# Writing the output projection of a hybrid decoder between the attention's steps, six matmuls at a time

## The chip, the core and the metric

The kernel runs on one core of a Trainium2 chip. The metric is device time in microseconds (us) of one launch. The engines are TensorE (PE in the rows; PEld are its weight loads), VectorE (DVE), ScalarE (ACT), GpSimd (POOL) and SyncE (SP), which issues the DMA transfers.

## The reference, cut to what matters

Two layers run over 2048 prompt tokens and 64 sample tokens, with D_MODEL 1024. In each layer four branches of width 256 (differential attention, spatial gating, convolution, gated recurrence) are gated, joined and sent through one 1024x1024 output projection. What the change touches is the prompt's attention and that projection:

```python
def _diff_attend(q1, q2, k1, k2, v, qpos, kpos, lam):
    def probs(q, k):
        s = jnp.einsum('bqhd,bkhd->bhqk', q, k) * scale
        return jax.nn.softmax(jnp.where(visible, s, NEG_BIG), axis=-1)
    p = probs(q1, k1) - lam * probs(q2, k2)
    return jnp.einsum('bhqk,bkhd->bqhd', p, v)
...
mixed = jnp.concatenate([o_a, o_b, o_c, o_d], -1) @ w_out[l]
y = _layer_norm(ALPHA * x + gate * mixed, ln_g[l], ln_b[l])
```

There are four heads, each with two score maps (q1 with k1, q2 with k2) of 32 columns and values of 64 columns.

## The kernel before, in words

A layer has two stages. The first computes the input projections and the other three branches and parks queries, keys, values and gated branches in device memory. The second is the attention stage: the prompt's causal attention, and the output projection beside it.

The 16 token tiles of 128 (t = 0 to 15) are taken in query blocks `qbs`: tiles 0-3, 4-7, 8-11, 12-13, 14-15. For each block `attention` goes over the four heads, and in a head over the block's tiles. One pass of tile t in one head is called a *row* here; there are 64 of them in a layer, 32 with t below 8 (short) and 32 long ones. A row does this:

- `attn_probs` takes each of the two maps in pieces of up to 1024 keys (one piece in a short row, two in a long one). A piece is two score matmuls into one of the two S buffers of PSUM (L669; the last piece adds the causal mask, L671), a maximum on VectorE (L673; a second piece joins maxima, L675), and the exponential on ScalarE (L677), which frees the S buffer. The sums are joined (L682, L684).
- the same function combines the two maps on VectorE: short operations on one number per token (L688, L689, L693), in a long row a scaling on ScalarE (L697), and then P1 + r P2 for each piece (L703 and, for the first piece of a long row, L698).
- `attn_value` transposes the combined piece in groups of four 128x128 blocks (L716), copies each group to SBUF on ScalarE (`ph`, L718) and multiplies it with the values into X (L721). It is called for a row after `attn_probs` of the following row. At a head's last tile it divides and normalises through a chain of short VectorE operations (`rsqrt`, L179 to L190), and stores the result.

`out_tile` is the output projection of one token tile. It loads gates and branches, multiplies (GpSimd L1340 for one half, VectorE L1346 for the other), splits the product into two fp32r parts (L110 on ScalarE, L172 on GpSimd), runs 48 matmuls in two groups of 24 into a z buffer (L1364 to L1366; there is one z buffer in this stage), and finishes with the residual, the norm and the store on VectorE, ScalarE and GpSimd (L1368 to L1382). The last block's two tiles (`last`) use the S buffers instead of z.

In the text of the program the four or two tiles of a block go through `out_tile` behind the attention of the next block, under `prio(KN['POUT'], ...)` with POUT = -500. The text isn't what the engines run: a list scheduler (`TCK = dict(schedule_with_timeline_sim=True)`) takes each engine's next instruction by the place in the text, which `prio` shifts, among those that its own timing model holds ready. `order` below stands for what it left in each engine's queue. Each queue runs in order.

Of the kernel before, what the change touches and what calls it, by code (L numbers as in the profile page):

```python
# [9 lines left out]
F32 = mybir.dt.float32  # L10
# [14 lines left out]
P = 128  # L25
# [43 lines left out]
def hymba_step_kernel(  # L69
# [9 lines left out]
    nc = tc.nc  # L79
# [19 lines left out]
    def prio(o, f, *a):  # L99
        if not o:  # L100
            return f(*a)
        with tc.high_priority(o):
            return f(*a)
# [514 lines left out]

        yield from for_tok(l, g, h, [(O_AV, 256)], consume)

    def attention(l, t0, nt, Lx, ap, act=None):

        S = scr[l]
        prev = None
        gq, oq = divmod(t0 * P, TG)
        nkc = -(-(t0 + nt) // 4)
        while len(pool.vst) < nkc:
            vt = (ap.v if pool.vst else ap.v0).tile([P, 4, 256], F32, name=nm("V"))
            load(vt, S.vs[len(pool.vst)].rearrange("(k p) c -> p k c", p=P))
            pool.vst.append(vt)  # L630
        vst = pool.vst
        for hd in range(4):
            rows = slice(hd * 64, (hd + 1) * 64)
            kst = []
            for c in range(0, nkc * 512, 512):
                gg, o = divmod(c, TG)
                kt = ap.k.tile([P, 2, 512], F32R, tag="K", name=nm("K"), bufs=NK)
                for q, part in enumerate((0, 0, 1, 1)):
                    load(kt[q * 32:(q + 1) * 32], S.ks[gg][part][rows, o:o + 512].rearrange("(m d) t -> d m t", m=2))
                kst.append(kt)  # L640
            qt = ap.q.tile([P, 2, 512], F32R, tag="Q", name=nm("Q"), bufs=2)
            for q, part in enumerate((0, 1, 0, 1)):
                load(qt[q * 32:(q + 1) * 32, :, 0:nt * P], S.qs[gq][part][rows, oq:oq + nt * P].rearrange("(m d) t -> d m t", m=2))
            ls = smp.tile([P, 4], F32, tag="ls", name=nm("ls"), bufs=3)
            acc = None
            for j in range(nt):
                pm = prio(KN['PPB'] if t0 else KN['PPB'], attn_probs, t0 + j, qt[:, :, j * P:(j + 1) * P], kst, ls[:, j:j + 1], Lx, ap)
                if prev is not None:
                    prio(KN['PAV'], prev)
                acc = Xt() if j == 0 else acc  # L650
                prev = (lambda *a: lambda: attn_value(*a, Lx, l, ap))(t0 + j, pm, vst, acc, ls, j, nt, hd, act)
        prev()

    def attn_probs(qi, qt, kst, l1, Lx, ap):

        nk = qi + 1
        npc = -(-nk // 8)
        stt = smp.tile([P, 16], F32, tag="stt", name=nm("stt"), bufs=3)
        Pm = []
        sizes = [min(8, nk - k0) * P for k0 in range(0, nk, 8)]  # L660
        col = lambda m, j: stt[:, m * 8 + j:m * 8 + j + 1]
        for m in range(2):
            pms = []
            for pc, n in enumerate(sizes):
                s = St()
                for o in range(0, n, 512):
# [11 lines left out]
                pms.append(p)  # L678
# [6 lines left out]
            Pm.append((pms, lt))  # L685
        (p1s, lt1), (p2s, lt2) = Pm
# [17 lines left out]
        return p1s  # L704

    def attn_value(qi, pm, vst, acc, ls, j4, nt, hd, act, Lx, l, ap):

        nk = qi + 1
        hs = slice(hd * 64, (hd + 1) * 64)
        for c in range(0, nk, 4):  # L710
            n = min(4, nk - c)
            p1 = pm[c // 8]
# [12 lines left out]
        if j4 < nt - 1:  # L725
# [591 lines left out]
    def out_tile(l, ti, O, last=False, act=None):  # L1317
# [7 lines left out]
        for half in (1, 0) if last else (0, 1):  # L1325
# [11 lines left out]
            for k0, k1 in ((2, 4), (0, 2)) if last and not half else ((0, 4),):  # L1337
# [9 lines left out]
                cpy('EOH', hi[:, cs], tmp[:, cs])  # L1347
                sub_lo(nc.vector if last and not half else pick('EOL'), lo[:, cs], tmp[:, cs], hi[:, cs])
                parts += [(O_K[half * 4 + k], f4(hi)[:, k, :], f4(lo)[:, k, :]) for k in range(k0, k1)]
        x = []  # L1350
        both = St() if last else None
        bs = smp.tile([P, 2, 6], F32, tag="obs", name=nm("obs"), bufs=2)
        for j in range(2):
# [9 lines left out]
            for i, (k, a, b) in enumerate(parts):  # L1363
                nc.tensor.matmul(po[0:M], a, wh[:, k, :], start=(i == 0), stop=False)  # L1364
                nc.tensor.matmul(po[0:M], a, wl[:, k, :], start=False, stop=False)  # L1365
                nc.tensor.matmul(po[0:M], b, wh[:, k, :], start=False, stop=(i == KT - 1))  # L1366
            t = O.op.tile([P, 512], F32, tag="xs", name=nm("t"), bufs=4)
            nc.vector.tensor_tensor(t[0:M], po[0:M], O.gate[0:M, js], ALU.mult)  # L1368
            nc.vector.scalar_tensor_tensor(xt[0:M], xt[0:M], ALPHA, t[0:M], op0=ALU.mult, op1=ALU.add)
# [30 lines left out]
    for l in range(DEPTH):  # L1400
# [92 lines left out]
        with ExitStack() as ctx2, \  # L1493
# [5 lines left out]
            if KN['WF']:  # L1499
                O = prio(KN['PW'], out_weights, l, op)  # L1500

            qbs = [(t, 4) for t in range(0, NT - 4, 4)] + ([(NT - 4, 2), (NT - 2, 2)], [(NT - 4, 3), (NT - 1, 1)], [(NT - 4, 2), (NT - 2, 1), (NT - 1, 1)])[KN['QB']]
            pool.vst = []
            for i, qb in enumerate(qbs):
                act = op.tile([P, qb[1], 256], F32, name=nm("act")) if i == len(qbs) - 1 else None
                if i and KN['OT'] == 0:
# [3 lines left out]
                if i == 0:  # L1510
                    if not KN['WF']:
                        O = prio(KN['PW'], out_weights, l, op)
                    out_gate(l, O, True)
                    out_tile(l, None, O)
                    out_gate(l, O, False)
                elif KN['OT']:
                    for t in range(qbs[i - 1][1]):
                        prio(KN['POUT'], out_tile, l, qbs[i - 1][0] + t, O)
            for t in range(qbs[-1][1]):
                out_tile(l, qbs[-1][0] + t, O, True, act[:, t])  # L1520
        pool.T2 = None
        if l < DEPTH - 1:
            zpool = ExitStack()
# [42 lines left out]
```

## Time and profile before

| what | us |
|---|---|
| time, median of 3 runs (3178.14 to 3194.91) | 3178.37 |
| the profiled execution: its time | 3180.86 |
| its span in the trace | 3179.1 |
| attention stage of layer 0, first to last score matmul | 1039 to 1566 |
| what follows it, into layer 1's first projections | 1566 to 1640 |
| attention stage of layer 1, first to last score matmul | 2592 to 3121 |
| what follows it, to the end | 3121 to 3179 |

Times inside the trace count from the span's start. Idle time in a row of the profile is the time that the engine stood still just before the instructions of that row, with what ended it behind the arrow.

### The profile page before, as it was taken

Reading aid. Unit: us, or ns where it says so; the run is one execution under the profiler, and the core shown is the slowest. Engines: PE = TensorE matmul, PEld = TensorE weight load, DVE = VectorE, ACT = ScalarE, POOL = GpSimd, SP = SyncE. Lnnn points to the kernel's source line nnn. Section 1 sums busy time; section 2 is a strip of 40 time slices with the busy share of each in tenths; the row PEclk is TensorE's granted clock in tenths of the full one; section 3 lists DMA queues with packets and bytes.
Section 4 is the critical chain, followed back from the end, with each engine's and each line's share of the span. In section 5 each row is a group of like instructions: output and inputs, shape, how many; then the busy total and the mean of one; then the engine's idle time right before and its main releaser. Section 6 shows DMA issues by size and latency. Waiting matters only on the chain. (4 is left out here: it accounts for less than half of the span.)

```text
span 3179.1 us, 56041 instructions
## 1 busy us (share of the span) xinstructions
PE 2821.6 (89%) x20888; PEld 2254.3 (71%) x20888; DVE 2272.4 (71%) x5280; ACT 1224.7 (39%) x2564; POOL 1140.0 (36%) x1173
## 2 busy tenths in 40 slices
PE   5999979898999898888889999888999989988896
PEld 3888866788866566656678888667897756665665
DVE  3667873377693788989857769534768758888896
ACT  3212213312213666676542122232122246657663
POOL 3344464433231223313343444653323431332232
PEclk7999989999999898999989999999999989998998
DMA  6222323322336754366332232242232254434552
GB/s 210 67 76 91 92 75 115 87 64 82 120 124 209 184 130 126 107 152 162 106 119 75 78 98 77 85 127 65 68 117 73 70 169 123 132 101 111 156 152 69
DMA packets 342593, 353.26 MB, mean 111 GB/s; under 512 B 58575, under 2 KB 248565, under 8 KB 342306
## 3 DMA queue, kind: packets, MB, share of 16 engines
q1 hardware_dynamic: 336178, 332.89, 36.5%
q0 software_dynamic: 6144, 16.79, 1.8%
q8 instruction: 166, 2.72, 0.4%
q14 instruction: 105, 0.86, 0.1%
HBM read 266.44 MB, written 83.33 MB: 110 GB/s over the span
## 5 line engine op out<-in xcount | busy, mean ns | idle before, releaser
L516 PE MATMUL z<-hh,wh 128*128 128x512 f32 (+1 forms) x1440 | 527.9, 367 | 27.4 <-DVE zs L195 25.0
L518 PE MATMUL z<-hh,wl 128*128 128x512 f32 (+1 forms) x1440 | 521.0, 362 | 0.0
L517 PE MATMUL z<-hl,wh 128*128 128x512 f32 (+1 forms) x1440 | 520.9, 362 | 0.0
L172 POOL TENSOR_TENSOR wl<-raw,wh 128x512 fp32r<-128x512 f32 x224 | 317.6, 1431 | 552.7 <-ACT wh L110 496.8
L507 PE MATMUL z<-wh,hh 128*128 128x256 f32 (+1 forms) x1360 | 399.6, 294 | 12.4 <-ACT wh L110 4.5
L1017 DVE SCALAR_TENSOR_TENSOR acc<-glu,cw,acc 128x512 f32<-128x512 f32 x480 | 403.2, 885 | 3.3
L677 ACT ACTIVATE P<-S,stt 128x1024 f32<-128x1024 f32 (+7 forms) x384 | 332.9, 868 | 178.9 <-DVE stt L673 124.0
L673 DVE TENSOR_REDUCE stt<-S 128x1 f32<-128x1024 f32 (+7 forms) x384 | 345.0, 905 | 70.9 <-PE S L671 55.2
L508 PE MATMUL z<-wl,hh 128*128 128x256 f32 (+1 forms) x1360 | 393.9, 290 | 0.6 <-POOL wl L172 0.6
L509 PE MATMUL z<-wh,hl 128*128 128x256 f32 (+1 forms) x1360 | 394.3, 290 | 0.0
L516 PEld LDWEIGHTS z<-hh,wh 128*128 128x128 f32 x1440 | 275.3, 191 | 91.7 <-DVE zs L195 30.1
L518 PEld LDWEIGHTS z<-hh,wl 128*128 128x128 f32 x1440 | 275.0, 191 | 45.2 <-issue 7.3
L517 PEld LDWEIGHTS z<-hl,wh 128*128 128x128 f32 x1440 | 275.4, 191 | 44.0 <-issue 7.7
L110 ACT CAST wh<-raw 128x512 fp32r<-128x512 f32 x224 | 134.2, 619 | 439.7 <-DMA raw<-in_w_in_dram 308.2
L669 PE MATMUL S<-K,Q 128*128 128x512 f32 (+3 forms) x640 | 229.5, 429 | 75.7 <-ACT P L677 66.3
L507 PEld LDWEIGHTS z<-wh,hh 128*128 128x128 f32 (+1 forms) x1360 | 261.9, 193 | 23.7 <-issue 5.7
L508 PEld LDWEIGHTS z<-wl,hh 128*128 128x128 f32 (+1 forms) x1360 | 261.7, 192 | 3.1 <-issue 0.9
L509 PEld LDWEIGHTS z<-wh,hl 128*128 128x128 f32 (+1 forms) x1360 | 261.4, 192 | 2.1 <-issue 0.3
L1364 PE MATMUL z<-woh,zs 128*128 128x512 f32 (+1 forms) x480 | 203.1, 423 | 24.4 <-ACT zs L110 12.4
L1366 PE MATMUL z<-woh,zs 128*128 128x512 f32 (+1 forms) x480 | 200.3, 417 | 10.2 <-POOL zs L172 10.0
L721 PE MATMUL X<-ph,V 128*64 128x128 f32 x2176 | 196.0, 293 | 10.2 <-ACT ph L718 9.7
L718 ACT COPY ph<-T 128x512 f32<-128x512 f32 (+2 forms) x320 | 161.0, 522 | 107.0 <-PE T L716 104.7
(374 smaller groups left out, 5505.5 us busy)
## 6 DMA issues: line engine op xcount, KB each, us to landing
raw<-in_w_in_dram SPq DMA_DIRECT2D x128, 256.0 KB
K<-kh SPq DMA_DIRECT2D x224, 128.0 KB
K<-kl SPq DMA_DIRECT2D x224, 128.0 KB
mw<-in_w_ada_dram SPq DMA_DIRECT2D x24, 1024.0 KB
raw<-in_w_in_dram SPq DMA_DIRECT2D x192, 128.0 KB
os<-gat SPq DMA_DIRECT2D x64, 256.0 KB
gat<-zs SPq DMA_DIRECT2D x48, 256.0 KB
os<-in_x_prompt_dram SPq DMA_DIRECT2D x32, 256.0 KB
```

Of the source, the lines that this page charges most:

```text
L172: eng.tensor_tensor(out, x, hi.bitcast(F32), ALU.subtract)
L507: nc.tensor.matmul(ps, hh[:, k, tok:tok + M], wh[:, k, :], start=(k == 0), stop=False)
L508: nc.tensor.matmul(ps, hh[:, k, tok:tok + M], wl[:, k, :], start=False, stop=False)
L509: nc.tensor.matmul(ps, hl[:, k, tok:tok + M], wh[:, k, :], start=False, stop=(k == KT - 1))
L516: nc.tensor.matmul(ps, wh[:, k, ms], hh[:, k, c0:c0 + n], start=(k == 0), stop=False)
L517: nc.tensor.matmul(ps, wh[:, k, ms], hl[:, k, c0:c0 + n], start=False, stop=False)
L518: nc.tensor.matmul(ps, wl[:, k, ms], hh[:, k, c0:c0 + n], start=False, stop=(k == KT - 1))
L669: nc.tensor.matmul(s[:, o:o + w], qt[:, m, :], kst[pc * 2 + o // 512][:, m, 0:w], start=True, stop=not diag)
L673: nc.vector.tensor_reduce(col(m, pc), s[:, :n], AX.X, ALU.max, negate=True)
L677: nc.scalar.activation(p[:, :n], s[:, :n], AF.Exp, bias=col(m, pc), scale=1.0, accum_out=l1 if m == 0 and npc == 1 else col(m, 2 + pc))
L1017: nc.vector.scalar_tensor_tensor(av, src(j), Lx.cw[:, c, j:j + 1], av, op0=ALU.mult, op1=ALU.add)
L1364: nc.tensor.matmul(po[0:M], a, wh[:, k, :], start=(i == 0), stop=False)
```

## The change

`attn_probs` is split. `attn_scores` does maxima, exponentials and sums, and yields after each piece; `attn_combine` yields after each combined piece; `attn_value` yields after each group of four blocks, and multiplies a group with the values only once the next group is transposed. A row's text now goes: one piece of its scores, one step of the row before (combination first, then values), and so on. The last row of a block is carried into the next block by `pool.pend`.

`out_tile` becomes a generator that yields after each half of its preparation and after every two of the eight k steps of a group, six matmuls: ten steps for a tile. `fill` is called behind each piece and each step and at a row's end, and takes up to three steps when fewer than `due` have been taken; `due` grows with t + 2.5 over the rows from t = 4 to 15. The tiles of a block become available when the first row of the next block is written. `prio` is gone from these calls.

```diff
+                sc = attn_scores(t0 + j, qt[:, :, j * P:(j + 1) * P], kst, ls[:, j:j + 1], Lx, ap)
+                steps = iter(prev) if prev else iter(())
+                for pm in sc:
+                    next(steps, None)
+                    fill(t0 + j, 0.2)
+                for _ in steps:
+                    fill(t0 + j, 0.2)
+                fill(t0 + j)
+                if j == 0:
+                    acc = Xt()
+                prev = chain(attn_combine(pm, Lx), attn_value(t0 + j, pm, vst, acc, ls, j, nt, hd, act, Lx, l, ap))
...
-            (nc.vector.tensor_copy if n <= KN['EPH'] else nc.scalar.copy)(ph[:, 0:n].rearrange("p k q -> p (k q)"), pt[:, 0:n * P])
-            for j in range(n):
-                e = (c + j) % 2
-                nc.tensor.matmul(acc[e * 64:(e + 1) * 64, j4 * P:(j4 + 1) * P], vst[c // 4][:, j, hs], ph[:, j, :],
-                                 start=(c + j < 2), stop=(c + j >= nk - 2), tile_position=(0, e * 64))
+            nc.scalar.copy(ph[:, 0:n].rearrange("p k q -> p (k q)"), pt[:, 0:n * P])
+            if todo:
+                values(*todo)
+            todo = (c, n, ph)
+            yield
+        values(*todo)
...
                 nc.tensor.matmul(po[0:M], b, wh[:, k, :], start=False, stop=(i == KT - 1))
+                if i % 2:
+                    yield
...
+            weight = lambda t: t + 2.5
+            F.total, F.weight = 10 * (NT - 1), sum(4 * weight(t) for t in range(4, NT))
+            def fill(t, share=None):
+                if t < 4:
+                    return
+                F.part = min(1.0, F.part + (share or 1.0))
+                due = F.total * (F.past + F.part * weight(t)) / F.weight
+                for _ in range(3):
+                    if F.gens and F.emitted < due:
+                        F.emitted += 1
+                        if next(F.gens[0], F) is F:
+                            F.gens.pop(0)
+                if share is None:
+                    F.past, F.part = F.past + weight(t), 0.0
+                    F.gens += F.wait
+                    F.wait = []
...
-                prio(KN['PATT'], attention, l, *qb, Lx, ap, act)
...
-                elif KN['OT']:
-                    for t in range(qbs[i - 1][1]):
-                        prio(KN['POUT'], out_tile, l, qbs[i - 1][0] + t, O)
+                    if i < len(qbs) - 1:
+                        F.wait += [out_tile(l, qb[0] + t, O) for t in range(qb[1])]
+                run(*F.gens)
```

No instruction is added or dropped on any engine, and their shapes stay. Line numbers shift: 669 to 680 (scores), 673 to 684 (maximum), 698 and 703 to 716 and 721 (combination), 716 to 742 (transposes), 721 to 731 (values), 1345 to 1372, and 1364-1366 to 1392-1394 (output).

Three places show how the queues move. The first is TensorE in layer 0 at tile 12 of the second head, from its first score matmul. S are scores, T transposes of probabilities P, X the values' sums. Before:

```order
L669 MATMUL S_14276<-K_14249,Q_14269 128x512
L669 MATMUL S_14276<-K_14254,Q_14269 128x512
L716 MATMUL T_14211<-cst,P_14137 128x128 x4
L716 MATMUL T_14222<-cst,P_14137 128x128 x4
L669 MATMUL S_14282<-K_14259,Q_14269 128x512
L721 MATMUL X_14171<-ph_14216,V_10307 64x128 x4
L716 MATMUL T_14233<-cst,P_14145 128x128 x4
L721 MATMUL X_14171<-ph_14227,V_11080 64x128 x4
L716 MATMUL T_14244<-cst,P_14145 128x128
L669 MATMUL S_14282<-K_14264,Q_14269 128x128
L671 LDWEIGHTS identb
L671 MATMUL S_14282<-cmaskb,identb 128x128
```

and with the change:

```order
L680 MATMUL S_14195<-K_14168,Q_14188 128x512
L680 MATMUL S_14195<-K_14173,Q_14188 128x512
L742 MATMUL T_14094<-cst,P_13898 128x128 x4
L742 MATMUL T_14121<-cst,P_13898 128x128 x4
L680 MATMUL S_14206<-K_14178,Q_14188 128x512
L731 MATMUL X_14049<-ph_14099,V_10307 64x128 x4
L742 MATMUL T_14142<-cst,P_13917 128x128 x4
L731 MATMUL X_14049<-ph_14126,V_10905 64x128 x4
L742 MATMUL T_14159<-cst,P_13917 128x128
L680 MATMUL S_14206<-K_14183,Q_14188 128x128
L682 LDWEIGHTS identb
L682 MATMUL S_14206<-cmaskb,identb 128x128
```

The twelve rows are the same instructions in the same order; no output matmul (z) stands between them in either.

The second is VectorE at the same row's combination, up to the piece of 1024 columns. `stt` holds one number per token, `sma`, `smaa` and `smay` belong to the chain that closes a head. Before:

```order
L673 TENSOR_REDUCE stt_14387<-S_14388 128x1
L684 SCALAR_TENSOR_TENSOR stt_14275<-stt_14275 128x1
L688 RECIPROCAL stt_14275<-stt_14275 128x1
L689 SCALAR_TENSOR_TENSOR stt_14275<-ls_14274,nlam_337,stt_14275 128x1
L673 TENSOR_REDUCE stt_14387<-S_14394 128x1
L693 TENSOR_TENSOR stt_14275<-stt_14275 128x1
L703 SCALAR_TENSOR_TENSOR P_14288<-P_14304,stt_14275,P_14288 128x640
L675 TENSOR_TENSOR stt_14387<-stt_14387 128x1
L673 TENSOR_REDUCE stt_14387<-S_14404 128x1
L698 SCALAR_TENSOR_TENSOR P_14280<-P_14280,stt_14275,P_14296 128x1024
```

and with the change:

```order
L711 TENSOR_TENSOR stt_14194<-stt_14194 128x1
L721 SCALAR_TENSOR_TENSOR P_14212<-P_14248,stt_14194,P_14212 128x640
L181 TENSOR_SCALAR smay_14313<-smai_14312 128x2
L183 TENSOR_TENSOR smaa_14314<-sma_14307,smay_14313 128x2
L189 SCALAR_TENSOR_TENSOR smaa_14314<-smaa_14314,smay_14313 128x2
L190 SCALAR_TENSOR_TENSOR smay_14313<-smaa_14314,smay_14313 128x2
L697 SCALAR_TENSOR_TENSOR ls_14193<-stt_14331 128x1
L183 TENSOR_TENSOR smaa_14314<-sma_14307,smay_14313 128x2
L189 SCALAR_TENSOR_TENSOR smaa_14314<-smaa_14314,smay_14313 128x2
L190 SCALAR_TENSOR_TENSOR smay_14313<-smaa_14314,smay_14313 128x2
L183 TENSOR_TENSOR smaa_14314<-sma_14307,smay_14313 128x2
L716 SCALAR_TENSOR_TENSOR P_14199<-P_14199,stt_14194,P_14227 128x1024
```

Before, one maximum of the next row's scores stands between the two combined pieces; with the change it is nine short operations of the closing chain and of the next row.

The third is TensorE behind the last score matmul of layer 0. Before:

```order
L669 MATMUL S_16186<-K_16032,Q_16042 128x512
L669 MATMUL S_16186<-K_16037,Q_16042 128x512
L671 LDWEIGHTS identb
L671 MATMUL S_16186<-cmaskb,identb 128x128
L716 MATMUL T_16202<-cst,P_16053 128x128 x4
L716 MATMUL T_16213<-cst,P_16053 128x128 x4
L1364 MATMUL z_16494<-woh_10883,zs_16439 128x512
L1365 MATMUL z_16494<-wol_10884,zs_16439 128x512
L1366 MATMUL z_16494<-woh_10883,zs_16440 128x512
L1364 MATMUL z_16494<-woh_10883,zs_16439 128x512
L1365 MATMUL z_16494<-wol_10884,zs_16439 128x512
```

and with the change:

```order
L680 MATMUL S_16246<-K_15994,Q_16004 128x512
L680 MATMUL S_16246<-K_15999,Q_16004 128x512
L682 LDWEIGHTS identb
L682 MATMUL S_16246<-cmaskb,identb 128x128
L1392 MATMUL S_16580<-woh_10833,zs_16555 128x512
L1393 MATMUL S_16580<-wol_10834,zs_16555 128x512
L1394 MATMUL S_16580<-woh_10833,zs_16556 128x512
L1392 MATMUL S_16580<-woh_10833,zs_16555 128x512
L1393 MATMUL S_16580<-wol_10834,zs_16555 128x512
L1394 MATMUL S_16580<-woh_10833,zs_16556 128x512
L1392 MATMUL S_16580<-woh_10833,zs_16555 128x512
```

Before, transposes and then output matmuls of an earlier tile (z) follow; with the change it is at once output matmuls of the last two tiles (in S buffers), and the earlier tile's 24 stand ahead of the last scores.

## Rows read from the trace of the kernel before

**Rows 1.** The page's first part: engine, busy us (share), instructions.

```profile
PE 2821.6 (89%) x20888; PEld 2254.3 (71%) x20888; DVE 2272.4 (71%) x5280; ACT 1224.7 (39%) x2564; POOL 1140.0 (36%) x1173
```

**Rows 2.** Windows over attention stages and what follows; header names the columns.

```profile
core 0: us, PE busy (x) PEld busy (x) DVE busy (x) ACT busy (x) POOL busy (x), PEclk, DMA share, GB/s
...
1039.00:1566.00 527.00, 459.39 (x2870) 331.77 (x2869) 466.62 (x1150) 347.42 (x754) 155.28 (x123) 0.94 0.53 138
1566.00:1640.00 74.00, 56.50 (x328) 45.73 (x327) 53.49 (x143) 30.67 (x69) 35.10 (x29) 0.87 0.48 144
...
2592.00:3121.00 529.00, 463.96 (x2883) 336.00 (x2882) 455.51 (x1156) 343.64 (x745) 149.33 (x116) 0.93 0.50 131
3121.00:3179.00 58.00, 35.34 (x185) 26.18 (x182) 34.69 (x98) 13.10 (x24) 7.49 (x6) 0.83 0.16 54
```

**Rows 3.** Groups by line, score matmuls, layer 0, then 1: count | busy, mean | idle.

```profile
L669 PE MATMUL S<-K,Q 128*128 128x512 f32 (+3 forms) x320 | 114.1, 429 | 36.9 <-ACT P L677 33.2 <-DMA K<-kl 2.6 <-DVE stt L673 0.6
...
L669 PE MATMUL S<-K,Q 128*128 128x512 f32 (+3 forms) x319 | 115.0, 429 | 38.8 <-ACT P L677 33.1 <-DMA K<-kl 5.4
```

**Rows 4.** Groups by line, maxima of the scores on VectorE, layer 0, then 1.

```profile
L673 DVE TENSOR_REDUCE stt<-S 128x1 f32<-128x1024 f32 (+4 forms) x192 | 172.3, 904 | 31.7 <-PE S L671 25.8 <-PE S L669 5.0
...
L673 DVE TENSOR_REDUCE stt<-S 128x1 f32<-128x1024 f32 (+7 forms) x190 | 171.3, 907 | 39.1 <-PE S L671 29.5 <-PE S L669 8.8
```

**Rows 5.** Timeline of TensorE near layer 0's last scores: start, us, what [idle].

```profile
1559.96 1.22 PE L669 MATMUL S<-K,Q 128*128 128x512 f32 x2 [2.88 <-ACT P L677]
...
1565.80 0.40 PE L1365 MATMUL z<-wol,zs 128*128 128x512 f32 x1
1566.03 0.40 PE L1366 MATMUL z<-woh,zs 128*128 128x512 f32 x1
```

**Rows 6.** Windows of 50 us in pairs; then L1364 alone there (PE, PEld busy).

```profile
1085.00:1135.00 50.00, 42.19 (x322) 29.58 (x323) 45.91 (x112) 39.06 (x89) 9.90 (x9) 1.00 0.50 127
1135.00:1185.00 50.00, 48.23 (x325) 36.42 (x324) 43.81 (x103) 30.30 (x64) 13.56 (x12) 1.00 0.50 133
1335.00:1385.00 50.00, 37.11 (x251) 25.62 (x249) 44.06 (x105) 38.17 (x79) 10.01 (x9) 0.90 0.47 117
1385.00:1435.00 50.00, 44.93 (x300) 32.70 (x301) 43.01 (x109) 35.51 (x75) 8.88 (x9) 1.00 0.63 156
...
2900.00:2950.00 50.00, 39.18 (x262) 27.07 (x261) 41.58 (x96) 41.27 (x87) 6.39 (x6) 0.88 0.51 123
2950.00:3000.00 50.00, 43.71 (x267) 31.82 (x266) 40.99 (x91) 29.67 (x61) 14.56 (x12) 0.98 0.59 153
...
1335.00:1385.00 50.00, 1.95 (x5) 0.78 (x5) 0.90 0.47 117
1385.00:1435.00 50.00, 9.87 (x24) 4.54 (x24) 1.00 0.63 156
...
2900.00:2950.00 50.00, 0.00 (x0) 0.00 (x0) 0.88 0.51 123
2950.00:3000.00 50.00, 12.68 (x31) 5.82 (x31) 0.98 0.59 153
```

**Rows 7.** Timelines of VectorE and of GpSimd around 1548 us.

```profile
1548.76 1.20 DVE L190 SCALAR_TENSOR_TENSOR smoy<-smoa,smoy 128x1 f32<-128x1 f32 x1
1549.99 0.16 DVE L183 TENSOR_TENSOR smoa<-smo,smoy 128x1 f32<-128x1 f32 x1
...
1547.45 2.50 POOL L172 TENSOR_TENSOR zs<-os,zs 128x512 fp32r<-128x512 f32 x2
```

**Rows 8.** Two short VectorE operations, layer 0: min/median/max ns; then the groups' means.

```profile
L675 DVE TENSOR_TENSOR stt<-stt x64: 134/151/1264, 1166.9 to 1563.6; 128x1 f32<-128x1 f32 x64
...
L689 DVE SCALAR_TENSOR_TENSOR stt<-ls,nlam,stt x63: 202/219/1325, 1041.4 to 1551.5; 128x1 f32<-128x1 f32 x63
...
L675 DVE TENSOR_TENSOR stt<-stt 128x1 f32<-128x1 f32 x64 | 21.9, 342 | 0.3
...
L689 DVE SCALAR_TENSOR_TENSOR stt<-ls,nlam,stt 128x1 f32<-128x1 f32 x63 | 20.9, 332 | 0.6
```

More of the change, by code (lines that the diff above doesn't have):

```diff
@@ L619, in a_v, with attention @@
         yield from for_tok(l, g, h, [(O_AV, 256)], consume)
-    def attention(l, t0, nt, Lx, ap, act=None):
+    def attention(l, t0, nt, Lx, ap, fill, act=None):
         S = scr[l]
-        prev = None
+        prev = pool.pend
         gq, oq = divmod(t0 * P, TG)
@@ L646, in attention, with attn_scores @@
             for j in range(nt):
[L647 to L654, printed above, removed]
+                sc = attn_scores(t0 + j, qt[:, :, j * P:(j + 1) * P], kst, ls[:, j:j + 1], Lx, ap)
[9 more added lines that the diff above has]
+                prev = chain(attn_combine(pm, Lx), attn_value(t0 + j, pm, vst, acc, ls, j, nt, hd, act, Lx, l, ap))
+        pool.pend = prev
+        if act is not None:
+            run(prev)
+            pool.pend = None
+    def attn_scores(qi, qt, kst, l1, Lx, ap):
         nk = qi + 1
@@ L658, in attn_probs @@
         stt = smp.tile([P, 16], F32, tag="stt", name=nm("stt"), bufs=3)
-        Pm = []
-        sizes = [min(8, nk - k0) * P for k0 in range(0, nk, 8)]
-        col = lambda m, j: stt[:, m * 8 + j:m * 8 + j + 1]
+        A = L()
+        A.col = col = lambda m, j: stt[:, m * 8 + j:m * 8 + j + 1]
+        A.sizes = sizes = [min(8, nk - k0) * P for k0 in range(0, nk, 8)]
+        A.p, A.l = [[], []], []
         for m in range(2):
-            pms = []
             for pc, n in enumerate(sizes):
@@ L703, in attn_probs, with attn_value, values @@
                 nc.vector.scalar_tensor_tensor(p1[:, :n], p2[:, :n], r, p1[:, :n], op0=ALU.mult, op1=ALU.add)
-        return p1s
-    def attn_value(qi, pm, vst, acc, ls, j4, nt, hd, act, Lx, l, ap):
+            yield
+    def attn_value(qi, A, vst, acc, ls, j4, nt, hd, act, Lx, l, ap):
         nk = qi + 1
         hs = slice(hd * 64, (hd + 1) * 64)
+        def values(c, n, ph):
+            for j in range(n):
+                e = (c + j) % 2
+                nc.tensor.matmul(acc[e * 64:(e + 1) * 64, j4 * P:(j4 + 1) * P], vst[c // 4][:, j, hs], ph[:, j, :],
+                                 start=(c + j < 2), stop=(c + j >= nk - 2), tile_position=(0, e * 64))
+        todo = None
         for c in range(0, nk, 4):
             n = min(4, nk - c)
-            p1 = pm[c // 8]
+            p1 = A.p[0][c // 8]
             o = (c % 8) * P
@@ L1349, in out_tile @@
                 parts += [(O_K[half * 4 + k], f4(hi)[:, k, :], f4(lo)[:, k, :]) for k in range(k0, k1)]
+            yield
         x = []
@@ L1500, in hymba_step_kernel @@
                 O = prio(KN['PW'], out_weights, l, op)
[L1502 to L1506, printed above, removed]
-                    for t in range(qbs[i - 1][1]):
-                        prio(KN['POUT'], out_tile, l, qbs[i - 1][0] + t, O)
-                prio(KN['PATT'], attention, l, *qb, Lx, ap, act)
[L1510 to L1515, printed above, removed]
-                elif KN['OT']:
-                    for t in range(qbs[i - 1][1]):
-                        prio(KN['POUT'], out_tile, l, qbs[i - 1][0] + t, O)
@@ L1519, in hymba_step_kernel @@
-            for t in range(qbs[-1][1]):
-                out_tile(l, qbs[-1][0] + t, O, True, act[:, t])
+            qbs = [(t, 4) for t in range(0, NT - 4, 4)] + [(NT - 4, 2), (NT - 2, 2)]
+            pool.vst, pool.pend = [], None
+            weight = lambda t: t + 2.5
+            F = L()
+            F.gens, F.wait, F.emitted, F.past, F.part = [], [], 0, 0.0, 0.0
+            F.total, F.weight = 10 * (NT - 1), sum(4 * weight(t) for t in range(4, NT))
[13 more added lines that the diff above has]
+                    F.wait = []
@@ new lines, in hymba_step_kernel, with sample @@
+            with ExitStack():
+                for i, qb in enumerate(qbs):
+                    act = op.tile([P, qb[1], 256], F32, name=nm("act")) if i == len(qbs) - 1 else None
+                    attention(l, *qb, Lx, ap, fill, act)
+                    if i == 0:
+                        O = out_weights(l, op)
+                        def sample():
+                            out_gate(l, O, True)
+                            yield from out_tile(l, None, O)
+                            out_gate(l, O, False)
+                        F.gens.append(sample())
+                    if i < len(qbs) - 1:
+                        F.wait += [out_tile(l, qb[0] + t, O) for t in range(qb[1])]
+                run(*F.gens)
+                for t in range(qbs[-1][1]):
+                    run(out_tile(l, qbs[-1][0] + t, O, True, act[:, t]))
```

12 lines of the change are left out of this document (9 added, 3 removed).

## The prediction

> **What bounds the kernel now.** I read the page's first part, then windows by stage, then who waits for whom in the two attention stages. TensorE is busy for 89% of the span [rows 1], but that average joins unlike stages. Outside the attention stages TensorE's queue is the same in both kernels but for a few places, behind layer 0's attention and in the middle of layer 1, where some matmuls swap; so only the two attention stages and what follows them can move: 527 and 529 us, with 74 and 58 us behind [rows 2].
>
> In these stages the reader is to see two engines close to full at once. TensorE is busy for 459.4 of 527.0 us and 464.0 of 529.0, VectorE for 466.6 and 455.5 [rows 2]. Between them runs a loop through the two S buffers: scores, maximum, exponential, and the buffer is free for the scores after next. TensorE's largest wait is that one: 33.2 and 33.1 us for the exponential [rows 3]. VectorE's largest wait is the loop's other side: 25.8 + 5.0 and 29.5 + 8.8 = 69.1 us for scores [rows 4]. One turn shows it: two score matmuls stand 2.88 us for an exponential [rows 5]. What shortens these waits is other TensorE work between one score piece and the next: transposes, values, and output matmuls, which follow each other at 0.23 us (1565.80 to 1566.03, rows 5). So the change is worth what it does to the order of this work, and no more, since no instruction goes.
>
> The granted clock was 0.94 and 0.93 of full in the two stages [rows 2], where TensorE stood still now and then; it is 1.00 and 0.98 in two stretches full of output matmuls, and 0.90 and 0.88 in the stretches nearly without them just ahead [rows 6].
>
> **The change part by part.** *Spreading the output matmuls.* I counted them in both queues row by row, a row beginning at its first score matmul. Before, they are missing in 22 of the 32 rows with t from 4 to 7 (11 in each layer), and in 12 of the 64 long rows (5 and 7). With the change it is again 22 (11 and 11), and 13 long rows (6 and 7). They also still run mostly in batches of 10 to 24, not of six. The first pair of queue rows above lies in such a gap, and there the queues are equal. So the text is spread and the queues are not: a tile's projection can't start before its block's heads are done and stored, and where it can start, the scheduler pulls it to the first hole. What a gap costs comes from pairs of neighbours. In the two late pairs the first holds 5 and 0 of the matmuls of L1364, a third of the output's, and the second 24 and 31 [rows 6]. TensorE is busy for 42.19 us of 50 and then 48.23, for 37.11 and 44.93, for 39.18 and 43.71 [rows 6]. The differences are 6.0, 7.8 and 4.5 us, 18 in all. The two late pairs (12.3 us) stand for the 12 long rows, so about 1 us a row: one row more is +1 us.
>
> *Scores ahead of combination.* For each of the 64 long rows I counted the maxima of later rows that stand ahead of its 1024-column combination in VectorE's queue. Before, the mean is 2.19 in layer 0 and 2.75 in layer 1; with the change, 2.22 and 2.63. The scheduler had already put scores ahead. The second pair of queue rows shows the one thing that differs at places: the short operations of a closing chain lie between the two combined pieces, where a maximum lay. I cost this at nothing as far as the 1024-column piece waits anyway for ScalarE's scaling of its other half (L697); if that cover is gone, it is in the next count.
>
> *The loop's slack.* For each score piece I added up the TensorE work between the end of the piece two before it and its own start: 0.23 us for 512 columns as in [rows 5], and 0.12 to 0.14 for a transpose or value matmul of 128 columns, which is my estimate from that (a quarter of the columns, and more than a quarter of the time). I took 2.8 us as the turn to be covered, the estimate from the wait of 2.88 us [rows 5]. What lacks to 2.8 sums to 210.7 us over both layers before and to 213.3 after, +1.2%. Priced by TensorE's 66.3 us of waiting [rows 3] that is +0.8 us. The same count on VectorE's queue (work between a maximum and the one two behind it, against 2.6 us, the time left for exponential and scores) goes from 45.9 to 53.2 us, +16%; priced by its 69.1 us of waiting [rows 4] that is +11 us. Both price one loop, so they aren't added, and either could be hidden by the other. I take +4, nearer to the first, because TensorE's waits alone hold up the score that the next maximum needs; 0.8 and 11 stay as ends.
>
> *The end of each stage.* Behind layer 0's last scores 24 output matmuls are gone (the third pair), 24 x 0.23 = 5.5 us; they run ahead of them now. TensorE's work behind that point shrinks by as much as the stage grows: nothing, unless they were cover. TensorE stood still for 74.0 - 56.5 = 17.5 us there [rows 2], so at worst the 5.5 us come on top. In layer 1 it is four matmuls, under 1 us.
>
> *The rest.* Loads of keys, gates and branches keep their number, and their order in SP's queue changes by a few places. Scores waited 2.6 + 5.4 us for keys [rows 3]; gone or doubled this is 8 us either way, and I take 0, since the keys' loads stay ahead of the same scores.
>
> The sum is +4 + 1 + 0 + 0 = +5 us on the profiled execution's 3180.9 us, and that lies 2.5 us above the median of the runs: 3178.4 + 5 = 3183 us. One thing in the trace speaks for so small a number: before the change the two layers already run the same work in unlike orders (gaps of 5 and 7 long rows, 2.19 and 2.75 maxima ahead), and their stages take 527 and 529 us [rows 2].
>
> **The rivals.** *The spreading works.* If the few moved batches land where TensorE is short of work, the gaps fill up. What they cost was 18 us (above), so the time would be 3178 - 18 = 3160 us. For it: in the gaps TensorE falls to 37 to 42 us of 50 and the clock to 0.90 and 0.88 [rows 6]. Against it: the gaps are still there in the queue, and VectorE is busy for 44.06 of 50 in the deepest, so half of the gain would run into VectorE. The Trainium skill has a rule of this kind (Perfetto Trace Analysis, Optimization Strategy): where a kernel has regimes with different most-contended engines, interleaving them may help. By that rule alone the change gains. The trace agrees that stretches with output matmuls use TensorE better; the queues say that the interleaving was already there.
>
> *VectorE and GpSimd get into each other's way more often.* A short VectorE operation that takes 0.16 us took 1.20 beside GpSimd's 128x512 subtraction [rows 7]. The groups show how often: L675's mean is 342 ns and its median 151, 64 x 0.191 = 12.2 us in layer 0; L689 has 332 against 219, 63 x 0.113 = 7.1 us [rows 8]. These two alone are some 19 us a layer, 39 in both. The change moves `out_tile`'s GpSimd work nearer to the rows (no -500 any more) and puts closing chains between combined pieces. Half as many meetings again cost +19 us, 3198 us; twice as many +39, 3217 us; it decides from 41% more (+16 us). Against it: GpSimd's work is unchanged and busy for only 155 of 527 us [rows 2]; half as many are as possible, and would give 3159. The Trainium skill (SBUF — State Buffer, the terms) describes the port pair that the two share as held for a whole instruction, so that the loser fully blocks. The 1.20 us beside a subtraction of 1.25 agree with it.
>
> **How the numbers follow.** A measurement of this kernel can tell a change from none at about 0.5%, 16 us. That the order changes and little else: 0.58, with 3165 to 3200 as its own range (-11 - 2 to +11 + 5.5 + 5); of it 0.45 falls within 0.5%, 0.05 below, 0.08 above. That gaps close or meetings get fewer: 0.21, all faster. That meetings get more: 0.21, all slower. So faster 0.26, the same 0.45, slower 0.29. The range goes from 18 us of gaps with 19 us of fewer meetings (3141) to twice as many meetings (3217).
>
> **What would show it.** In the changed kernel's trace: score matmuls waiting for exponentials, 60 to 75 us over both stages (the spreading works: under 45); VectorE's maxima waiting for scores, 65 to 85 us; the stages at 520 to 536 us each; gaps with TensorE below 42 of 50 us at about the same tiles, t = 4 to 7 and the first heads of block 12-13; L675's and L689's successors at means of 0.3 to 0.35 us (the second rival: over 0.45). The prediction is wrong if both stages move the same way by over 8 us. That would mean that the new order has an effect which my counts, made from places in the queues and not from times, can't see.

## The result, and the profile after

The changed kernel takes 3203.12 us (median of 12 runs, 3194.34 to 3224.38) against 3178.26 for the kernel before (12 runs beside them, 3173.81 to 3194.91). The ratio is 1.0081, with a 95% interval of 1.0064 to 1.0098: the change makes the kernel slower, by 26 us (20 to 31). The profiled execution took 3199.69 us with a span of 3196.6, that is 17.5 us more than the span before.

The page's first part, and the windows that answer to [rows 2] (the stages start and end elsewhere now):

```profile
PE 2846.4 (89%) x20888; PEld 2258.9 (71%) x20888; DVE 2281.1 (71%) x5280; ACT 1228.0 (38%) x2564; POOL 1114.0 (35%) x1173
...
core 0: us, PE busy (x) PEld busy (x) DVE busy (x) ACT busy (x) POOL busy (x), PEclk, DMA share, GB/s
1031.00:1584.00 553.00, 476.08 (x2899) 340.90 (x2897) 471.98 (x1162) 349.17 (x752) 162.15 (x128) 0.93 0.51 133
1584.00:1657.00 73.00, 54.64 (x301) 42.31 (x301) 47.98 (x132) 30.86 (x71) 27.35 (x26) 0.81 0.43 131
2602.00:3139.00 537.00, 468.99 (x2854) 335.42 (x2854) 462.45 (x1141) 340.94 (x739) 144.55 (x116) 0.93 0.50 129
3139.00:3197.00 58.00, 36.75 (x213) 27.41 (x213) 33.27 (x113) 16.14 (x31) 7.51 (x6) 0.87 0.16 53
```

The reader is to see that the instruction counts are the same, that layer 0's stage grew from 527 to 553 us and layer 1's from 529 to 537, and that the stretches behind them did not. The windows are cut as in [rows 2]; they are not quite "first to last score matmul", as the table of times before calls them. By the starts of those matmuls themselves the stages ran from 1039.4 to 1560.6 and from 2584.6 to 3120.2 us, and now run from 1031.4 to 1578.9 and from 2594.7 to 3138.5: 521.2 and 535.6 us before, 547.5 and 543.8 now. Two stretches whose work did not grow run the other way in this one execution: the first score matmul comes at 1031 us instead of 1039, though TensorE's and VectorE's queues are the same up to it, and from layer 0's last score to layer 1's first it is 8 us less, where the 24 moved output matmuls are gone. So +26, +8, -8 and -8 make about the 17.5 us, and how much one execution wanders is told at the end.

In the two stages TensorE now stands still for 76.9 + 68.0 = 144.9 us. Before it was 67.6 + 65.0 = 132.6 [rows 2]: 12 us more. From the first to the last score of each layer, the clock's records have TensorE at the lower of its two levels (1.2 GHz) for 157 us, before for 131. Matmuls at that level are about half as fast (a place is shown below), so these 26 us account for up to another 13 or so of this one execution, by my estimate. The moved matmuls are 5.5.

Who waits, in groups by line (count | busy, mean | idle): TensorE's scores and third output matmul in layer 0, the same in layer 1; then VectorE's maxima in layer 0 with two short operations, and the maxima in layer 1. They answer to [rows 3, 4, 8].

```profile
L680 PE MATMUL S<-K,Q 128*128 128x512 f32 (+3 forms) x320 | 115.8, 437 | 34.4 <-ACT P L688 30.5 <-DMA K<-kl 3.5
L1394 PE MATMUL z<-woh,zs 128*128 128x512 f32 (+1 forms) x237 | 98.7, 416 | 10.5 <-POOL zs L172 10.4
...
L680 PE MATMUL S<-K,Q 128*128 128x512 f32 (+3 forms) x319 | 118.5, 440 | 39.4 <-ACT P L688 30.2 <-DMA K<-kl 6.7 <-ACT zs L110 1.7
L1394 PE MATMUL z<-woh,zs 128*128 128x512 f32 (+1 forms) x233 | 95.9, 412 | 9.0 <-POOL zs L172 9.0
...
L684 DVE TENSOR_REDUCE stt<-S 128x1 f32<-128x1024 f32 (+4 forms) x192 | 172.4, 905 | 43.8 <-PE S L682 28.4 <-PE S L680 14.8
L707 DVE SCALAR_TENSOR_TENSOR stt<-ls,nlam,stt 128x1 f32<-128x1 f32 x63 | 20.1, 319 | 0.6
L686 DVE TENSOR_TENSOR stt<-stt 128x1 f32<-128x1 f32 x64 | 18.0, 281 | 0.3
...
L684 DVE TENSOR_REDUCE stt<-S 128x1 f32<-128x1024 f32 (+7 forms) x190 | 171.0, 906 | 46.1 <-PE S L682 37.8 <-PE S L680 7.7
```

TensorE's wait for exponentials went down a little, 66.3 to 60.7 us. VectorE's wait for scores went up, from 69.1 to 43.2 + 45.5 = 88.7. So scores come later for a reason other than their wait for exponentials. One new reason stands in the rows of L1394: output matmuls that wait for GpSimd's low halves (`zs`, line 172). The view of that tile's GpSimd instructions in layer 0 ends with who waited for them (us, times); before:

```profile
  PEld z L1366: 5.7, 9
  PE z L1366: 3.3, 3
```

and after:

```profile
  PEld z L1394: 14.0, 13
  PE z L1394: 10.4, 10
```

Over both layers TensorE's matmuls (the PE lines) wait 9.4 us before and 19.4 after. What one such wait does is seen in the changed kernel's timeline of TensorE, then of GpSimd (start, us, what, [idle before]), with windows over the same place:

```profile
1306.89 0.74 PE L680 MATMUL S<-K,Q 128*128 128x512 f32 x2 [0.57 <-ACT P L688]
1307.46 0.43 PE L1392 MATMUL z<-woh,zs 128*128 128x512 f32 x1
1307.73 0.40 PE L1393 MATMUL z<-wol,zs 128*128 128x512 f32 x1
1307.97 0.49 PE L680 MATMUL S<-K,Q 128*128 128x512 f32 x1
1308.31 0.23 PE L682 MATMUL S<-cmaskb,identb 128*128 128x128 bf16 x1
1310.49 0.50 PE L1394 MATMUL z<-woh,zs 128*128 128x512 f32 x1 [1.96 <-POOL zs L172]
...
1313.61 0.63 PE L1394 MATMUL z<-woh,zs 128*128 128x512 f32 x1
1314.04 0.63 PE L1392 MATMUL z<-woh,zs 128*128 128x512 f32 x1
1314.46 0.62 PE L1393 MATMUL z<-wol,zs 128*128 128x512 f32 x1
1314.89 0.89 PE L680 MATMUL S<-K,Q 128*128 128x512 f32 x3
...
1307.94 1.27 POOL L1367 TENSOR_TENSOR os<-os,os 128x512 f32<-128x512 f32 x1 [6.70 <-DMA os<-catT]
1309.17 2.51 POOL L172 TENSOR_TENSOR zs<-os,zs 128x512 fp32r<-128x512 f32 x2
...
1308.00:1311.50 3.50, 1.54 (x7) 1.11 (x7) 3.50 (x9) 2.35 (x6) 3.50 (x3) 1.00 0.27 70
1311.50:1314.90 3.40, 3.40 (x10) 2.62 (x9) 3.23 (x14) 1.47 (x4) 0.18 (x1) 0.50 0.03 7
```

The first two output matmuls run, the third needs a low half that GpSimd starts only at 1309.17, and TensorE's queue stands for 1.96 us with the next scores (1314.89) behind it. GpSimd was late because it had itself stood idle for 6.70 us until a load of branches (`os<-catT`) landed: here the tile's loading, and not only its arithmetic, came too late. The granted clock then falls to 0.50 from 1311.5 to 1314.9: output matmuls follow each other at 0.43 us instead of 0.23.

### The profile page after: what moved, and what is told of

Read it like the earlier page. It is cut to its first block, busy times and chain, and to the rows that moved or that the text cites. A ratio compares the mean times of both kernels' runs of the same rounds, so it can differ in the third digit from the quotient of the medians.

```text
span 3196.6 us, 56049 instructions
## 1 busy us (share of the span) xinstructions
PE 2846.4 (89%) x20888; PEld 2258.9 (71%) x20888; DVE 2281.1 (71%) x5280; ACT 1228.0 (38%) x2564; POOL 1114.0 (35%) x1173
## 5 line engine op out<-in xcount | busy, mean ns | idle before, releaser
L172 POOL TENSOR_TENSOR wl<-raw,wh 128x512 fp32r<-128x512 f32 x224 | 311.0, 1402 | 548.0 <-ACT wh L110 500.6
L680 PE MATMUL S<-K,Q 128*128 128x512 f32 (+3 forms) x640 | 234.7, 438 | 73.8 <-ACT P L688 60.7
L110 ACT CAST wh<-raw 128x512 fp32r<-128x512 f32 x224 | 134.2, 619 | 413.4 <-DMA raw<-in_w_in_dram 281.1
L1394 PE MATMUL z<-woh,zs 128*128 128x512 f32 (+1 forms) x480 | 200.1, 417 | 20.0 <-POOL zs L172 19.9
L731 PE MATMUL X<-ph,V 128*64 128x128 f32 x2176 | 203.9, 298 | 10.2 <-ACT ph L744 9.1
```

The lines of the kernel that those rows point to most:

```text
L172: eng.tensor_tensor(out, x, hi.bitcast(F32), ALU.subtract)
L680: nc.tensor.matmul(s[:, o:o + w], qt[:, m, :], kst[pc * 2 + o // 512][:, m, 0:w], start=True, stop=not diag)
```

## The experiments

Each ratio is to runs of the kernel before on the same chip, with a 95% interval; us are the ratio times the median of those runs. The first line is the result above (3178.26 us). The others come from three sets on three chips: four experiments beside 3195.07 us, four beside 3199.98 and four beside 3192.02, in the order of the table.

| run | ratio | us against before |
|---|---|---|
| the change | 1.0081 (1.0064 to 1.0098) | +26 |
| fill alone | 1.0060 (1.0039 to 1.0081) | +19 |
| attention alone | 0.9995 (0.9977 to 1.0013) | -2 |
| change, values not later | 1.0087 (1.0063 to 1.0112) | +28 |
| change, steps at -500 | 1.0047 (1.0029 to 1.0064) | +15 |
| change, low halves last | 1.0042 (1.0018 to 1.0065) | +13 |
| before, low halves last | 1.0023 (1.0001 to 1.0045) | +7 |
| change, steps at -2000 | 1.0043 (1.0020 to 1.0065) | +14 |
| change, preparation at +2000 | 1.0035 (1.0014 to 1.0055) | +11 |
| change, matmuls on ready data | 1.0117 (1.0075 to 1.0158) | +37 |
| before, matmuls on ready data | 1.0032 (1.0012 to 1.0052) | +10 |
| before, preparation at +2000 | 1.0013 (0.9992 to 1.0035) | +4 |
| change, preparation +2000, matmuls -2000 | 1.0022 (0.9999 to 1.0046) | +7 |

**Which part.** *Fill alone*: `attention` and what it calls are those of before, with calls of `fill` between the rows' halves; the tile of the sample tokens goes through `fill` too.

```diff
+                for _ in range(2):
+                    fill(t0 + j, 0.2)
                 if prev is not None:
                     prio(KN['PAV'], prev)
+                for _ in range(2):
+                    fill(t0 + j, 0.2)
+                fill(t0 + j)
```

> The attention of before, row by row as before, with the changed out_tile: a generator taken in steps of six matmuls by fill, at the priority of the rest instead of -500. Theory A (the new order inside the attention costs the time: scores, combination and values taken alternately, values a group later, the last row carried over): within 6 us of before. Theory B (the output work, now at the same priority and in small steps, gets ahead of scores and holds up the loop of scores, maximum and exponential): +15 to +30 us, that is the whole of the loss, with layer 0's attention stage near 547 us as in the changed kernel. Theory C (only the two together cost): within 6 us here and in the run of attention alone.

Measured +19 us (12 to 26), layer 0 from first to last score 544.9 us: theory B. The lower clock is not needed for it: the mean granted clock over these 7 runs is 0.944, as over the 19 of the kernel before beside them. So the clock's part worked out above belongs to that execution and is not shown to be a part of the loss in general.

*Attention alone*: `fill` does nothing, and the tiles are written behind the next block as before.

```diff
+            fill = lambda t, share=None: None
...
-                        F.gens.append(sample())
-                    if i < len(qbs) - 1:
-                        F.wait += [out_tile(l, qb[0] + t, O) for t in range(qb[1])]
-                run(*F.gens)
+                        run(sample())
+                    else:
+                        for t in range(qbs[i - 1][1]):
+                            prio(-500, run, out_tile(l, qbs[i - 1][0] + t, O))
```

> The changed attention alone (split scores, combination, values a group later, the last row carried into the next block); the output tiles are written whole behind the next block at priority -500, as before. Theory A: +15 to +30 us, the whole loss. Theory B: within 6 us of before. Theory C: within 6 us here and in the run of the fill alone.

Measured -2 us (-7 to +4). Theories A and C fall: the split of the attention costs nothing that can be told, and the output work alone costs 19 us (12 to 26) of the change's 26 (20 to 31), all of it within the intervals. The windows over the stages, of the fill alone and then of attention alone:

```profile
1043.00:1589.00 546.00, 470.28 (x2882) 337.88 (x2880) 477.36 (x1151) 345.39 (x745) 156.20 (x124) 0.93 0.52 134
2623.00:3153.00 530.00, 461.64 (x2857) 331.94 (x2857) 451.36 (x1140) 344.50 (x744) 150.12 (x119) 0.94 0.50 129
```

```profile
1047.00:1570.00 523.00, 463.23 (x2877) 333.94 (x2876) 459.34 (x1141) 343.72 (x745) 159.06 (x124) 0.94 0.53 138
2591.00:3132.00 541.00, 472.22 (x2878) 336.95 (x2878) 456.81 (x1142) 344.04 (x742) 150.33 (x120) 0.93 0.49 128
```

From first to last score the two stages take 521.2 and 535.6 us before, 544.9 and 528.6 with the fill alone, and 522.4 and 540.0 with attention alone. So in this execution the fill lengthens layer 0's stage and not layer 1's. With attention alone TensorE stands still for 59.8 + 68.8 = 128.6 us; before, cut in the same way, it is 67.6 + 66.6 = 134.2.

*Values not later*: `values(c, n, ph)` right behind its transposes, no `todo`.

> The changed kernel, but each group of four blocks is multiplied with the values in the step that transposes it, as before, not one step later. If the later values are what costs (TensorE goes 86 times from a transpose to a value matmul in the two stages, 60 before, and a switch takes 0.20 us instead of 0.11): 8 to 25 us less than the changed kernel, that is 0 to +17 us against before. If the delay of values costs nothing: the changed kernel's +25 us, within 6.

Measured +28 us (20 to 36), the changed kernel's loss over again beside other runs of the kernel before: the later values cost nothing that can be told.

*Steps at -500*: `prio(-500, next, F.gens[0], F)` in `fill`.

> The changed kernel with fill's steps at priority -500, as the output tiles had before; the text stays spread. Theory B in the form that the lost priority is what costs: within 8 us of before. Theory A: the changed kernel's +25 us, within 6, since the order inside the attention is untouched.

Measured +15 us (9 to 20), neither number. The lost priority is part of it and not all. TensorE waits for low halves 23.8 us here, 27.2 in the fill alone, and 10.2 in attention alone. From that came theory D (TensorE stands at low halves that GpSimd has not finished, and scores stand behind them), against E (the place of the output work in the queues costs, ready or not).

**Readiness or place.** *Low halves last*, in the changed kernel and in the one before:

```diff
+            mms = [s for k, a, b in parts for s in ((a, wh, k), (a, wl, k))] + [(b, wh, k) for k, a, b in parts]
+            for i, (s, w, k) in enumerate(mms):
+                nc.tensor.matmul(po[0:M], s, w[:, k, :], start=(i == 0), stop=(i == 3 * KT - 1))
...
```

> The changed kernel, but in each group of 24 output matmuls the 16 that read the high half stand first and the 8 that read the low half, which GpSimd makes last, stand at the end; the same matmuls, steps of six. Theory D (the output work is spread, so a tile is prepared just ahead of its matmuls, and TensorE, whose queue is in order, stands at low halves that GpSimd has not finished: 9 us over both stages before, 19 in the changed kernel, 27 and 27 in the fill alone and in the run without later values, 24 in the run at priority -500): the wait for GpSimd under 6 us in both stages, and the time within 10 us of before. Theory E (the place of the output work costs, not its readiness: steps at the same priority get ahead of scores and hold up their loop): +18 to +28 us against before, as the changed kernel.

> The kernel before with the same order inside a group of output matmuls, high half first. Theory D: it waits little for low halves (9 us over both stages), so 0 to -9 us against before. Theory E: no change within 6 us.

Measured +13 (6 to 21) and +7 us (0 to 14); neither theory has both. The wait for low halves is gone, but the waits for ScalarE's high halves take its place, 22.9 us in the changed kernel (7.4 there without this edit) and 16.1 in the one before (6.8). A batch of output matmuls now stands at its high halves instead of its low ones. The two kernels lie nearer to each other, 6 us instead of 26, with intervals that overlap.

*Steps at -2000*, and *preparation at +2000* (the two preparing steps of a tile, matmul steps at 0):

```diff
+                        if prio(2000 if F.k < 2 else 0, next, F.gens[0], F) is F:
```

> The changed kernel with fill's steps at priority -2000: the text stays spread, but in the scheduler's choice the output work stands behind some 2000 instructions of attention. Theory E: the loss goes on falling with the priority (+0.81% at 0, +0.47% at -500), to within 8 us of before. Theory D: it falls only if the wait for low halves falls too; at +15 us or more if that wait stays at 20 us or more.

> The changed kernel with the two preparing steps of each tile at priority +2000 and the matmul steps at 0 as in the changed kernel. Theory D: preparation comes earlier where buffers allow it, the wait for low halves falls, and the time with it: +5 to +18 us against before. Theory E: the changed kernel's +25 us or more, since more work stands ahead of scores.

Measured +14 and +11 us. The priority takes about half of the loss and no more, and its wait for low halves stays at 1.4 + 20.1 us: nearer to D than to E, though the interval holds both. Earlier preparation takes over half of it, with the wait down to 16.1 us: against E, and in the direction that D has. The sizes do not fit D alone: the wait falls by 3 us from 19.4, the cost by some 15.

*Matmuls on ready data*, in both kernels:

```diff
-                nc.tensor.matmul(po[0:M], a, wh[:, k, :], start=(i == 0), stop=False)
+                nc.tensor.matmul(po[0:M], wh[:, k, 0:M], wh[:, k, :], start=(i == 0), stop=False)
...
```

> The changed kernel, but the output matmuls read a block of the output weights, which is there all the time, in place of the prepared halves zs; the preparation is still done, and nothing of TensorE waits for it. Its output is not the layer's; only the time is of use. Theory D (TensorE, in order, stands at halves that are not ready, and scores stand behind them): the difference to the kernel before with the same edit is within 8 us. Theory E (the place of the output work in the queues costs, ready or not): +18 us or more against that kernel.

> The kernel before with the same edit: output matmuls that read weights in place of the prepared halves (the output is not the layer's). Theory D: 0 to -16 us against before, as it stood 9 us for GpSimd's halves and 7 for ScalarE's. Theory E: within 6 us of before.

Measured +37 us (24 to 50) and +10 (4 to 17), 27 apart: D forecast under 8, so D as the whole cause is not borne out, since without any wait for the prepared halves the two kernels differ as much as with it. The pair is no clean test of it, for the edit also moves the matmuls in the queues. Both kernels got slower. TensorE's wait for exponentials is longer; the changed kernel, layer 0 and 1:

```profile
L680 PE MATMUL S<-K,Q 128*128 128x512 f32 (+3 forms) x320 | 119.2, 448 | 53.8 <-ACT P L688 48.0 <-DMA K<-kl 3.7 <-DVE stt L684 1.9
...
L680 PE MATMUL S<-K,Q 128*128 128x512 f32 (+3 forms) x320 | 117.8, 438 | 57.3 <-ACT P L688 46.8 <-DMA K<-kl 9.1 <-ACT cn L110 0.7
```

and the kernel before:

```profile
L669 PE MATMUL S<-K,Q 128*128 128x512 f32 (+3 forms) x319 | 118.2, 443 | 49.8 <-ACT P L677 43.1 <-DMA K<-kl 5.7 <-ACT ph L718 0.6
...
L669 PE MATMUL S<-K,Q 128*128 128x512 f32 (+3 forms) x320 | 115.0, 431 | 43.1 <-ACT P L677 38.4 <-DMA K<-kl 2.6 <-ACT cn L110 0.7
```

That is 94.8 and 81.5 us, where the kernels themselves have 60.7 and 66.3. Output matmuls that can run early run out early: stretches of over 10 us without one, added up over both stages, are 461 us in the changed kernel with this edit and 446 in the kernel before with it, against 342 and 331 without it. In them no output matmul covers the loop's waits. Here the clock fell too: its mean over the runs is 0.938 and 0.940, where the kernel before beside them has 0.944. As a share of the span that is, by my estimate, up to 20 and 12 us. And gaps look cheap: the kernel before got 115 us more of them, while its waits for the halves (9.4 + 6.8 us) went, and lost 10 us by both together. So the 11 us more of gaps that the change brings can hardly be its 26.

*Preparation at +2000* in the kernel before, and both priorities together in the changed one (+2000 for preparation, -2000 for matmuls):

> The kernel before with the two preparing steps of each output tile at priority +2000 and its matmuls at -500 as before. Theory D: the halves are ready earlier still, 0 to -12 us against before. Theory E: preparation ahead of scores costs or does nothing, 0 to +10 us.

> The changed kernel, spread text, with the preparing steps at priority +2000 and the matmul steps at -2000. Theory D: the wait for low halves falls to 10 us or less over both stages, as before, and the time is within 8 us of before. Theory E: like the run with all steps at -2000, +0.43%, 14 us, within 6.

Measured +4 us (-3 to 11) and +7 (0 to 15). The first tells nothing apart. The second takes away most of the loss, though the wait for low halves is still 16.0 us, not the 10 or less that D wanted; its interval holds both theories' times. No version is shown to beat the kernel before.

## Why the range held and the reason was missed

*The sum.* It said +5 us and the change costs 26 (20 to 31). 3203 lies above the likeliest case's own range (to 3200), and inside the whole range only because that range reaches up to the second rival's 3217; that rival's mechanism did not come (below), so this is luck. The likeliest outcome, the same within 0.5%, had 0.45; slower, which came, had 0.29. The step that failed is "about 1 us a row: one row more is +1 us", the term for spreading the output matmuls. Measured alone, that part costs 19 us. The term asked where output matmuls are missing. It did not ask whether those that are there can start, and what stands behind them when they can't. At the place shown above, a batch that began 2 us too early held up the scores behind it. That this is what the 19 us consist of is likely and not shown.

*The loop's slack*, +4 with 0.8 and 11 as ends. As far as this count was about the attention's order, that measures -2 us (-7 to +4): its low end fits, and pricing VectorE's waits at 11 does not. One of its inputs was too high: 0.12 to 0.14 us for a value matmul, where in the trace before these follow each other at 0.06 us on the mean at the full clock (transposes at 0.11). So what lacks is more than 210.7 and 213.3 us, in both kernels. *Scores ahead of combination* at 0 fits the same run, which does not measure it by itself.

*The gaps.* The reading that the text is spread and the queues are not was right: the long stretches without output matmuls add up to 331 us before and 342 after. Two windows near those of [rows 6], without any matmul of line 1392:

```profile
1330.00:1380.00 50.00, 36.00 (x217) 24.66 (x216) 40.67 (x108) 37.30 (x82) 5.68 (x5) 0.80 0.31 79
2900.00:2950.00 50.00, 34.49 (x221) 23.43 (x221) 40.38 (x102) 37.61 (x82) 5.67 (x5) 0.79 0.38 94
```

TensorE is busy for 36.0 and 34.5 us of 50, where [rows 6] has 37.1 and 39.2 in the deepest. So the first rival (3160 us, the spreading works) did not come. The Trainium skill says that interleaving regimes with different most-contended engines may help (Perfetto Trace Analysis, Optimization Strategy). This interleaving did not: the fill alone measures +0.60%.

*Collisions of VectorE and GpSimd*, the second rival, gives the right time (3198 to 3217) by a mechanism that the rows deny. L675's and L689's successors have means of 281 and 319 ns in layer 0 (342 and 332 in [rows 8]), and 283 and 335 in layer 1 (266 and 299 before), where the rival wanted over 450. Whoever looked at the time alone would have called it confirmed.

*The end of layer 0's stage* at nothing: the 24 matmuls are 5.5 us, and the stretch to layer 1's first score got 8 us shorter while the stage grew, as the step says; in one execution 8 us can also be chance.

*What would show it.* Waits for exponentials 60.7 us (60 to 75 expected): right. Maxima waiting for scores 88.7 (65 to 85), stages of 553 and 537 us (520 to 536): missed. The prediction's own sign of failure, both stages moving the same way by over 8 us, came (26 and 8.2 from first to last score): "an effect which my counts, made from places in the queues and not from times, can't see" is what it was. That sign rests on one execution, and layer 1's 8.2 us alone would prove nothing (see the end).

**What stays open.** That the way the output work is written costs the time, and the split of the attention does not, is shown. That lower priority and earlier preparation each take about half of it away is measured, in other sets of runs than the change itself and with intervals that touch its own or nearly do. How the cost divides between standing at halves not yet prepared and output matmuls in the wrong place is not shown: taking the first away moves the matmuls as well.

The profiles together speak for the first, one execution each. Take the runs that keep both the matmuls' order and their operands, and set the wait for low halves over both stages beside the cost, both in us: 9.4 and 0 (before), 10.2 and -2 (attention alone), 12.1 and +4 (before, preparation at +2000), 16.0 and +7 (both priorities), 16.1 and +11, 21.5 and +14, 23.8 and +15, 27.2 and +19 (fill alone), 27.2 and +28 (values not later). The two rise together, and only the change itself, 19.4 and +26, stands out. In six of the nine changed runs here, the layer whose wait grew more over before is also the one whose stage grew more. The fill alone waits 16.1 us in layer 0, and that stage is 544.9 us, 24 above before. With the steps at -500 and -2000 it is layer 1 that waits (20.2 and 20.1 us, layer 0 3.6 and 1.4), and layer 1 that is long: 548.8 and 548.5 us, 13 above before. So the fill does not lengthen layer 0's stage by nature. This is a correlation; no run moved the wait alone.

## What to carry to other kernels

Before filler work is woven into a tight loop, look at how far ahead its operands are ready, not only at where the loop has holes: on an engine whose queue is in order, filler that is late holds up the loop, and filler that is early is gone when the hole comes. A count from places in a queue says whether the order changed, and here it said so rightly for the attention; it can't price a wait for another engine. Where a change has two parts, time each alone before explaining either.

## What the runs showed of the hardware that was not expected

A stall can cost more than its length: after the 1.96 us above, TensorE ran at 0.50 of its clock for 3.4 us, eight matmuls at 0.43 us instead of 0.23, some 1.5 us more. That is one place: the runs of the fill alone lose their time at an unchanged mean clock (0.944).

The same queues take different times. The change, attention alone and the steps at -500 have the same TensorE and VectorE queues as the kernel before up to layer 0's first score, and reach it at 1031.4, 1047.6, 1052.5 and 1039.4 us in their profiled executions. Part of that may be the chip: the medians of the unchanged kernel ran from 3178 to 3200 us over the four sets of runs, which were not all made on one chip. But on one chip too the fill alone, attention alone, values not later and the steps at -500, with these same queues, reach it at 1043.6, 1047.6, 1046.0 and 1052.5 us. So 8 us in one stage of one execution, the prediction's own threshold, is no evidence; the medians beside the kernel before, on the same chip, are.
